# Storing the second images of the last four pairs from GpSimd's queue instead of ScalarE's

## The chip, the cores and the metric

The kernel runs on one core of a Trainium2 chip. The metric is the device time of one execution in microseconds (us); a smaller number is better. A core has five engines that work side by side: TensorE (PE, matrix products), VectorE (DVE), ScalarE (ACT), GpSimd (POOL) and SyncE (SP), and sixteen DMA engines that carry data between the device memory and the on-chip memory. SyncE, ScalarE and GpSimd can each issue DMAs, each on a queue of its own; in the profile q1 is SyncE's queue, q10 is ScalarE's, and q0, of the kind called software_dynamic, is GpSimd's.

## The reference

The kernel computes a 3x3 convolution with padding 1 on 16 images of 64 channels and 64x64 pixels, with 128 output channels, in float32:

```python
x_pad = np.pad(x, ((0, 0), (0, 0), (1, 1), (1, 1)))
for b, co, ci, kh, kw in ...:      # 16, 128, 64, 3, 3
    output[b, co] += weight[co, ci, kh, kw] * x_pad[b, ci, kh:kh+h, kw:kw+w]
```

x is 16.8 MB and the output is 33.6 MB; the weights are 0.3 MB.

## The kernel before

**Tiling.** Two images make a pair: image 0 of the pair has its 64 channels in partitions 0 to 63, image 1 in partitions 64 to 127. There are eight pairs (p = 0 to 7). A pair is worked off in four blocks (blk), each of eight row pairs, that is sixteen output rows.

**Arithmetic.** Output rows are made two at a time, j and its neighbour, with a scheme that shares one product between the two. The sums of each pair of input rows are formed beforehand (the tile ss, function sums, line 62). TensorE then computes three groups per block (function group, line 141): U, from ss with the centre weights G1; A, from single rows with G21 and G0; and Bt, from single rows with G01 and G2. ScalarE copies U out of the accumulators (the tile ut, line 182). VectorE adds A and ut into the even output rows (line 190), and Bt and ut into the odd ones (line 193). The result tile of one image of a pair is ot, 128 output channels by 64 by 64 float32, 2 MB.

**Input.** x of pairs 0 to 2 is loaded as float32 by SyncE's queue into tiles of the same pool as ot, and converted to f16 on chip by ScalarE and GpSimd. x of pairs 3 to 7 is loaded by GpSimd's queue (function load, line 56), with the conversion to f16 made by the DMA; these loads are issued early, two at about 12 us and three at about 27 us. The row sums of pairs 1 to 7 run on GpSimd (line 131), and those of pair p+1 are issued at the head of pair p's turn in the loop. The pool of ss has three buffers.

**Output.** Image 0 of a pair is stored by SyncE's queue (line 195) as soon as its last block is added. Image 1 is put on a list, held, and stored by ScalarE's queue behind ScalarE's next two copies of U (lines 184 and 185), or behind the loop (lines 198 and 199). Pairs 0 and 7 store in halves of 32 rows (pair 0 its image 0 only); all other images are stored whole. The pool of ot and of the three float32 loads has seven buffers, so a tile takes over the buffer of a tile seven earlier, after that one's store has landed.

**Order.** Instructions in keep(...) stay in the order of the program on their engine. That holds for all instructions of GpSimd and ScalarE named here. An instruction that waits, a DMA issue too, therefore holds up what stands behind it on its engine.

Of the kernel before, what the change touches and what calls it, by code (L numbers as in the profile page):

```python
# [13 lines left out]
def kernel(  # L14
# [6 lines left out]
    nc = tc.nc  # L21
# [6 lines left out]
    keep = tc.keep_in_program_order  # L28
# [27 lines left out]
    def load(p):  # L56
        xs[p] = xpool.tile([128, H, W], F16, tag="xs", name="xs")
        keep(nc.gpsimd.dma_start(xs[p], x_rows[128 * p : 128 * p + 128, :, :]))  # L58
# [3 lines left out]
    def sums(eng, p, src, lo, n):  # L62
        if p not in ss:
            ss[p] = spool.tile([128, H // 2, W], F16, tag="ss", name="ss")
        v = src.rearrange("p (j i) c -> p j i c", i=2)
        keep(
            eng.tensor_add(  # L67
                ss[p][:, lo : lo + n, :], v[:, lo : lo + n, 0, :], v[:, lo : lo + n, 1, :]
            )
        )  # L70
# [26 lines left out]
    def cast(copy, p, src, lo, hi):  # L97
        keep(copy(xs[p][:, lo:hi, :], src[:, lo:hi, :]))  # L98
# [21 lines left out]
    cuts_of = [(halves, whole)] + [(whole, whole)] * (NP - 2) + [(halves, halves)]  # L120

    def store(eng, p, b2, ot, lo, hi):
        return eng.dma_start(
            out_rows[2 * p + b2, :, lo:hi, :],
            ot.rearrange("p j i c -> p (j i) c")[:, lo:hi, :],
        )

    for p in range(NP):
        if p + 1 < NP:
            for lo in (0, 16):  # L130
                sums(nc.gpsimd, p + 1, raws.get(p + 1, xs[p + 1]), lo, 16)
                if (p, lo) == (1, 16):
                    for q in range(5, NP):
                        load(q)
        ots = [
            opool.tile([128, H // 2, 2, W], F32, tag="ot", name="ot") for _ in range(2)
        ]
        for blk in range(4):
            j0 = blk * RB

            def group(wi_rows):

                tiles = [
                    psum.tile([128, RB, W], F32, tag="acc", name="acc") for _ in range(2)
                ]
                n = 3 * len(wi_rows)
                i = 0
                for wi, off in wi_rows:
                    for kw in (1, 0, 2):
                        c_lo, c_hi = max(0, 1 - kw), min(W, W + 1 - kw)  # L150
                        for b2 in range(2):
                            p0 = 64 * b2
                            lo, hi = j0, j0 + RB
                            if off is None:
                                rhs = ss[p][p0 : p0 + 64, lo:hi, c_lo + kw - 1 : c_hi + kw - 1]
                            else:
                                while 2 * lo + off < 0:
                                    lo += 1
                                while 2 * (hi - 1) + off > H - 1:
                                    hi -= 1  # L160
                                first = 2 * lo + off
                                last = 2 * (hi - 1) + off
                                rhs = xs[p][
                                    p0 : p0 + 64,
                                    first : last + 1 : 2,
                                    c_lo + kw - 1 : c_hi + kw - 1,
                                ]
                            nc.tensor.matmul(  # L168
                                tiles[b2][:, lo - j0 : hi - j0, c_lo:c_hi],
                                Wt[p0 : p0 + 64, wi, kw, :],  # L170
                                rhs,
                                start=i == 0,
                                stop=i == n - 1,
                            )
                        i += 1
                return tiles

            U = group([(G1, None)])
            us = []
            for b2 in range(2):  # L180
                ut = upool.tile([128, RB, W], F32, tag="ut", name="ut")
                keep(nc.scalar.copy(ut, U[b2]))  # L182
                us.append(ut)
            while held and (p, blk) != (1, 0):
                keep(store(nc.scalar, *held.pop(0)))
            for piece in later.get((p, blk), ()):
                cast(nc.scalar.copy, *piece)
            A = group([(G21, 1), (G0, -1)])
            for b2 in range(2):
                nc.vector.tensor_add(ots[b2][:, j0 : j0 + RB, 0, :], A[b2], us[b2])  # L190
            Bt = group([(G01, 0), (G2, 2)])
            for b2 in range(2):
                nc.vector.tensor_add(ots[b2][:, j0 : j0 + RB, 1, :], Bt[b2], us[b2])  # L193
            if blk in cuts_of[p][0]:
                store(nc.sync, p, 0, ots[0], *cuts_of[p][0][blk])
            if blk in cuts_of[p][1]:
                held.append((p, 1, ots[1], *cuts_of[p][1][blk]))
    while held:
        keep(store(nc.scalar, *held.pop(0)))
# [30 lines left out]
```

## Time and profile before

| | us |
|---|---|
| Time of three runs: median (lowest to highest) | 126.29 (126.21 to 126.46) |
| Time of the profiled execution | 126.58 |
| Its span in the profile | 124.8 |
| First matmul on x to the last one | 9.83 to 112.6 |
| Last addition of VectorE ends | 113.98 |

DMA issues, by queue: engine, count, KB of each, and the median time from issue to landing.

```profile
out_dram<-ot ACTq DMA_DIRECT2D x7, 2048.0 KB, 19.4
out_dram<-ot SPq DMA_DIRECT2D x6, 2048.0 KB, 19.1
x<-in_x_dram SPq DMA_DIRECT2D x3, 2048.0 KB, 12.3
xs<-in_x_dram POOLq DMA_DIRECT2D x5, 1024.0 KB, 21.7
out_dram<-ot SPq DMA_DIRECT2D x4, 1024.0 KB, 11.8
out_dram<-ot ACTq DMA_DIRECT2D x2, 1024.0 KB, 10.9
```

How to read the profile: the page gives for each engine its busy time, its share of the span and the number of its instructions. The span is cut into 40 slices, and a digit is a slice's busy share in tenths, with 9 for 90% and more. A DMA queue's line gives packets, MB, and the time of its packets as a share of sixteen engines' span. The table by stretch has, for a stretch of the span, the busy time of each engine with its number of instructions in brackets, TensorE's granted clock, the DMA engines' busy share, and GB/s. In an order of time a line is start, duration, engine, line of the code, operation, output and input; in square brackets stands the idle time before it and what ended that. A name with a q (ACTq, SPq) is the engine's instruction queue, where DMA issues are recorded. The trace also has a record of each DMA packet, with its queue, start, duration and size; where the text speaks of packet records, it means these.

### The profile page before, as it was taken

How to read it: one execution, taken by the hardware profiler on the slowest of the kernel's cores; microseconds unless marked ns; L12 is line 12 of the kernel's file. 1: busy time of each engine (PE TensorE's matmuls, PEld its weight loads, DVE VectorE, ACT ScalarE, POOL GpSimd, SP SyncE). 2: the span in 40 equal slices, each digit the busy share in tenths (PEclk: the TensorE clock that was granted, in tenths of full speed). 3: DMA queues.
4: the chain of work that ended last, by engine and by line, in shares of the span. 5: the costliest groups of instructions: out<-in, count | busy, mean ns of one | idle time of the engine just before them, and what ended most of it. 6: DMA issues, size and time to landing. Idle time of an engine off the chain costs nothing.

```text
span 124.8 us, 2427 instructions
## 1 busy us (share of the span) xinstructions
PE 107.6 (86%) x984; PEld 50.2 (40%) x984; DVE 84.5 (68%) x135; ACT 46.5 (37%) x78; POOL 37.5 (30%) x28
## 2 busy tenths in 40 slices
PE   0598999999999999999999999999999999991000
PEld 0543444444444444444444444444444444440000
DVE  1009987878877887877777778777877787775000
ACT  4108649966663333333333333333333333330000
POOL 2209790899594003900066000930000000000000
PEclk9999999999999999999999999999999999999855
DMA  5999999999999999999999999999999999999991
GB/s 131 394 431 452 441 302 229 284 284 289 365 349 336 341 381 349 365 344 336 373 362 365 334 347 415 441 436 420 415 447 415 436 410 441 431 402 418 425 407 53
DMA packets 4042, 45.52 MB, mean 365 GB/s; under 512 B 448, under 2 KB 448, under 8 KB 576
## 3 DMA queue, kind: packets, MB, share of 16 engines
q1 hardware_dynamic: 2016, 23.36, 45.0%
q10 hardware_dynamic: 1296, 16.78, 31.7%
q0 software_dynamic: 720, 5.24, 20.5%
q8 instruction: 7, 0.11, 0.3%
q14 instruction: 3, 0.02, 0.0%
HBM read 17.07 MB, written 33.55 MB: 406 GB/s over the span
## 4 chain that ended last, share of the span: by engine, by line
PE 81%; DMA 6%; DVE 2%; issue 1%; DVEq 0%; SPq 0%
PE acc L168 81%; DMA x<-in_x_dram 6%; DVE ot L190 1%; DVE ss L67 1%; DVE ot L193 0%; DVEq L225 0%; SPq L41 0%; DVEq L190 0%
## 5 line engine op out<-in xcount | busy, mean ns | idle before, releaser
L168 PE MATMUL acc<-xs,Wt 64*128 64x504 f16 (+3 forms) x768 | 87.2, 373 | 0.0
L168 PEld LDWEIGHTS <-Wt 64*128 64x128 f16 x960 | 47.3, 94 | 56.2 <-issue 1.1
L182 ACT COPY ut<-acc 128x512 f32<-128x512 f32 x64 | 34.4, 589 | 56.9 <-issue 39.0
L190 DVE TENSOR_TENSOR ot<-acc,ut 128x512 f32<-128x512 f32 x64 | 41.2, 685 | 20.8 <-PE acc L168 18.4
L193 DVE TENSOR_TENSOR ot<-acc,ut 128x512 f32<-128x512 f32 x64 | 41.1, 683 | 0.0
L67 POOL TENSOR_TENSOR ss<-xs 128x1024 f16<-128x1024 f16 x10 | 21.1, 2127 | 32.6 <-DMA xs<-in_x_dram 20.5
L168 PE MATMUL acc<-ss,Wt 64*128 64x504 f16 (+1 forms) x192 | 26.1, 377 | 0.6 <-DVE ss L67 0.6
L98 ACT CAST xs<-x 128x1024 f16<-128x1024 f32 (+1 forms) x10 | 10.5, 1070 | 3.5 <-DMA x<-in_x_dram 3.5
L67 POOL TENSOR_TENSOR ss<-x 128x1024 f16<-128x1024 f32 x4 | 9.4, 2365 | 4.3 <-DMA x<-in_x_dram 4.3
L67 DVE TENSOR_TENSOR ss<-x 128x512 f16<-128x512 f32 x4 | 3.3, 867 | 7.8 <-DMA x<-in_x_dram 7.8
L85 PE MATMUL wp<-ident,w 128*64 128x128 f16 x18 | 1.3, 328 | 4.4 <-POOL w L52 4.4
L98 POOL CAST xs<-x 128x1024 f16<-128x1024 f32 (+1 forms) x2 | 3.0, 1519 | 4.7 <-DMA x<-in_x_dram 4.7
L91 PE MATMUL warm<-blank 128*128 128x400 f32 x6 | 3.6, 757 | 0.0
L85 PEld LDWEIGHTS <-w 128*64 128x64 f16 x18 | 1.1, 210 | 4.4 <-POOL w L52 4.4
L58 POOL DMA_DIRECT2D xs<-in_x_dram x5 | 2.9, 579 | 0.0
L91 PEld LDWEIGHTS warm<-blank 128*128 128x128 f32 x6 | 1.7, 304 | 1.4 <-issue 1.2
L92 ACT CAST Wt<-wp 128x384 f16<-128x384 f32 x1 | 0.5, 479 | 3.1 <-PE wp L85 3.1
L92 ACT ACT_TABLE_LOAD x1 | 1.3, 1283 | 0.7 <-PEq L214 0.7
L52 POOL CAST w<-w_raw 128x576 f16<-128x576 f32 x1 | 0.7, 662 | 2.4 <-DMA w_raw<-in_weight_dram 2.4
L88 DVE MEMSET blank<- 128x400 f32 x1 | 0.4, 392 | 0.9 <-PEq L214 0.9
L103 ACT CAST Wt<-wp 128x384 f16<-128x384 f32 x1 | 0.5, 478 | 0.5 <-DVE Wt L95 0.5
L94 DVE TENSOR_TENSOR Wt<-wp,Wt 128x384 f16<-128x384 f32 x1 | 0.6, 550 | 0.0
(8 smaller groups left out, 1.9 us busy)
## 6 DMA issues: line engine op xcount, KB each, us to landing
out_dram<-ot ACTq DMA_DIRECT2D x7, 2048.0 KB, 19.4
out_dram<-ot SPq DMA_DIRECT2D x6, 2048.0 KB, 19.1
x<-in_x_dram SPq DMA_DIRECT2D x3, 2048.0 KB, 12.3
xs<-in_x_dram POOLq DMA_DIRECT2D x5, 1024.0 KB, 21.7
out_dram<-ot SPq DMA_DIRECT2D x4, 1024.0 KB, 11.8
out_dram<-ot ACTq DMA_DIRECT2D x2, 1024.0 KB, 10.9
w_raw<-in_weight_dram SPq DMA_DIRECT2D x1, 288.0 KB, 2.9
```

Source lines behind the costliest of these rows:

```text
L52: keep(nc.gpsimd.tensor_copy(w16, w_raw))
L58: keep(nc.gpsimd.dma_start(xs[p], x_rows[128 * p : 128 * p + 128, :, :]))
L67: eng.tensor_add(ss[p][:, lo : lo + n, :], v[:, lo : lo + n, 0, :], v[:, lo : lo + n, 1, :])
L85: nc.tensor.matmul(wp[q : q + 64, k * CO : k * CO + CO], w16[:, t::9], ident)
L91: nc.tensor.matmul(warm[:, 0:400], blank[:, 0:128], blank)
L92: keep(nc.scalar.copy(wrow(G1), wps[1]))
L94: keep(nc.vector.tensor_sub(wrow(G21), wps[2], wrow(G1)))
L98: keep(copy(xs[p][:, lo:hi, :], src[:, lo:hi, :]))
L168: nc.tensor.matmul(tiles[b2][:, lo - j0 : hi - j0, c_lo:c_hi], Wt[p0 : p0 + 64, wi, kw, :], rhs, start=i == 0, stop=i == n - 1,)
L182: keep(nc.scalar.copy(ut, U[b2]))
L190: nc.vector.tensor_add(ots[b2][:, j0 : j0 + RB, 0, :], A[b2], us[b2])
L193: nc.vector.tensor_add(ots[b2][:, j0 : j0 + RB, 1, :], Bt[b2], us[b2])
```

## The change

From pair 4 on, the store of image 1 is issued by GpSimd at the place in the program where its last block is added, instead of being put on the list for ScalarE. It is kept in program order on GpSimd: the store of pair 4 stands behind the row sums of pair 5 and ahead of those of pair 6, and the store of pair 5 ahead of the row sums of pair 7. Five DMAs move: three whole images (pairs 4, 5, 6) and the two halves of pair 7. ScalarE keeps the four stores of pairs 0 to 3.

```diff
             if blk in cuts_of[p][0]:
                 store(nc.sync, p, 0, ots[0], *cuts_of[p][0][blk])
-            if blk in cuts_of[p][1]:
+            if blk in cuts_of[p][1] and p >= 4:
+                keep(store(nc.gpsimd, p, 1, ots[1], *cuts_of[p][1][blk]))
+            elif blk in cuts_of[p][1]:
                 held.append((p, 1, ots[1], *cuts_of[p][1][blk]))
     while held:
         keep(store(nc.scalar, *held.pop(0)))
```

## The prediction

> **What bounds the kernel now.** I read the head of the page first, then the DMA queues, then the busy time by stretch, and last the order of time around a pair's end and around the kernel's end.
>
> ```profile
> span 124.8 us, 2427 instructions
> PE 107.6 (86%) x984; PEld 50.2 (40%) x984; DVE 84.5 (68%) x135; ACT 46.5 (37%) x78; POOL 37.5 (30%) x28
> DMA  5999999999999999999999999999999999999991
> q1 hardware_dynamic: 2016, 23.36, 45.0%
> q10 hardware_dynamic: 1296, 16.78, 31.7%
> q0 software_dynamic: 720, 5.24, 20.5%
> ```
>
> TensorE is busy for 86% of the span, but the DMA row has a nine in every slice from the second to the last but one, and the queues' shares sum to 45.0 + 31.7 + 20.5 = 97.2% of sixteen engines' time. q1 is SyncE's queue, q10 ScalarE's, q0 GpSimd's. The table by stretch says where this decides:
>
> ```profile
> core 0: us, PE busy (x) PEld busy (x) DVE busy (x) ACT busy (x) POOL busy (x), PEclk, DMA share, GB/s
> 47.00:75.00 28.00, 28.00 (x266) 13.00 (x264) 21.96 (x36) 8.89 (x18) 8.41 (x4) 1.00 1.02 354
> 77.00:100.00 23.00, 23.00 (x218) 10.63 (x216) 18.06 (x30) 7.52 (x14) 4.21 (x2) 1.00 1.01 431
> ...
> 114.00:118.00 4.00, 0.00 (x0) 0.00 (x0) 0.00 (x0) 0.00 (x0) 0.00 (x0) 0.95 1.01 426
> 118.00:121.00 3.00, 0.00 (x0) 0.00 (x0) 0.00 (x0) 0.00 (x0) 0.00 (x0) 0.50 1.01 426
> 121.00:123.40 2.40, 0.00 (x0) 0.00 (x0) 0.00 (x0) 0.00 (x0) 0.00 (x0) 0.50 0.38 157
> ```
>
> The last two columns are the DMA engines' busy share and the GB/s that they moved. (The loads on q0 are counted at their f16 size, half of what is read, so 354 and 431 GB/s are nearly the same pace.) From 114 us no compute engine works, yet the DMA engines are full until 121. The chain of waits ends at the last addition at 113.98 us; what follows, to 124.8, is a backlog of stores. So this kernel ends when its bytes are through, about 1.4 us after its last packet: the trace's packet records put that one at 123.34 us.
>
> The order of time at a pair's end (here pair 4), and GpSimd's order around it:
>
> ```profile
> 74.28 1.28 DVE L193 TENSOR_TENSOR ot<-acc,ut 128x512 f32<-128x512 f32 x2
> ...
> 74.98 0.33 SPq L123 DMA_DIRECT2D out_dram<-ot  x1
> 75.59 0.34 ACTq L123 DMA_DIRECT2D out_dram<-ot  x1
> ```
>
> ```profile
> 26.93 1.63 POOL L58 DMA_DIRECT2D xs<-in_x_dram  x3
> ...
> 63.38 4.21 POOL L67 TENSOR_TENSOR ss<-xs 128x1024 f16<-128x1024 f16 x2 [10.37 <-PE acc L168]
> 77.98 4.21 POOL L67 TENSOR_TENSOR ss<-xs 128x1024 f16<-128x1024 f16 x2 [10.40 <-DMA xs<-in_x_dram]
> ```
>
> The first image's store leaves at 74.98, the second's at 75.59, 0.03 us after the pair's last addition. GpSimd's last two rows are the row sums of pairs 6 and 7.
>
> **The change part by part.** The sum is made against the profiled execution: 126.58 us, of which 124.8 are span and 1.8 lie around it. The median of the runs shown is 126.29, which is 0.29 less; I carry differences over to it.
>
> *Five store issues leave ScalarE*, 0.34 us each. After each of them ScalarE sat idle for 2.1 us before its next copy (78.08 after 75.59, 90.89 after 88.39, 103.70 after 101.20). Worth: 0. That cover is the wait for TensorE's next block, and nothing in the change touches it.
>
> *Five store issues come to GpSimd.* The five loads that it issues took 0.579 us on average (535 to 704 ns), so 2.9 us in all, on an engine busy for 30%. What matters is what stands behind them. The store of pair 4 waits for 75.56 and stands ahead of pair 6's sums, which ran at 63.38: they move to 75.56 + 0.6 = 76.2 and end at 80.4. Pair 5's store waits for 88.37 and stands ahead of pair 7's sums: 89.0 to 93.2 instead of 77.98 to 82.2. TensorE reads them first at 86.83 and 99.64 (the first matmuls on ss of those pairs). Both have 6.4 us to spare, so 0; with that cover gone, each us would hold up TensorE by one. Pairs 6 and 7's stores have no sums behind them.
>
> *Output buffers.* The transfers issued by 75.6 us all land by 94.51 now. With the same bytes on the same engines, another order between queues can't finish the whole later, and the last two tiles that need a freed buffer are first written at 101.75. Worth 0, with 7 us to spare.
>
> *Issue to first packet.* With the engines full, a queue that was empty starts late whoever owns it. From the packet records: ScalarE's queue 26.96 to 30.62 (3.66 us) and 101.20 to 105.17 (3.97), SyncE's 106.96 to 111.28 (4.32), GpSimd's 12.05 to 15.91 (3.86, descriptor writing included). So a moved store starts between 0.5 us earlier and 0.2 us later than on ScalarE's queue. It costs only where an engine runs dry. In the records the number of packets in flight never falls under 16 between 3 and 121 us. The tightest spot is the end: the last half image needs 8 packets of 0.309 us per engine, 2.47 us, and the engines finish between 121.28 and 123.34, so they are out of other work between 118.8 and 120.9. Its first packet can come at 113.98 + 4.32 = 118.3. Covered on every engine, by 2.6 us on the one that sets the end: 0.
>
> *The packets themselves.* 512 packets of 16 KB (or their worth) change queue, 32 per engine. Upper bound: by the queues' shares, q0's packets took 0.205 x 16 x 124.8 / 640 = 640 ns each and q10's 0.317 x 1996.8 / 1024 = 618 ns per 16 KB, 22 ns more, which gives 32 x 22 ns = 0.70 us. But q0's loads also convert to f16, and packets overlap. The pace tells more: with three queues sharing, ScalarE's stores land 14.67 us apart (56.93, 71.60), that is 24 packets per engine at 611 ns; with two queues, 9.71 us (91.69, 101.40) for 16, at 607. If q0 alone is charged with the 4 ns, 8 of its packets cost 0.10 us and 32 cost 0.40. Lower bound: nothing, if the conversion explains it; the bytes are the same, so below nothing is excluded for this term. By rate of bytes read, in the packet records, 47 to 75 us ran at 427.0 GB/s and 77 to 100 us at 429.1, 0.5% apart; over the 44 us in which stores would be on q0 that is 0.2 us. I take half of it, 0.1, as the rate is nearer to "no difference" than to 0.70.
>
> *The end.* SyncE waits for all landings; after the last one 1.4 us pass. Unchanged.
>
> Sum: 0 + 0 + 0 + 0 + 0.1 = +0.1, so 126.68 against the profiled 126.58, and **126.4 us** against the median of 126.29: the same, if no change is taken as within 0.2% (0.25 us), about what a measurement of this kernel can resolve.
>
> **The rivals.** *A queue that is slow when it is alone* (slower). Load 3 is the only transfer that ever had engines to itself on q0. While it shared with SyncE's load its packets took 625 ns; from 19.2 to 22.7 us, when that load had ended, 60 of them took 758 ns on average, up to 1132. ScalarE's queue, nearly alone from 108 to 111 us, kept a median of 611. If the cause is the software queue, it returns where q0 will be alone: now q10 is alone for about 28 engine-us at 108 to 111 (38.1 busy less 9.9 of q1 beside it) and 15 at 118 to 123.4, 2.7 us per engine. At 758/611, 24% more: +0.65 us, **127.0**. If it is the conversion, or reading x, nothing. It decides from about 0.9 us per engine with q0 alone. One stretch is thin evidence, and q0's later packets at 28 to 30 us, when they held 12 of 16 engines between 8 KB stores, took 624.
>
> The Trainium skill ("DMA: Bandwidth & Descriptors", section Bandwidth) gives 425 GB/s for a 16 MB load issued from GpSimd; by that a software queue alone would not be slow, and no run here shows an unconverted GpSimd transfer.
>
> *Two slow engines set the end* (slower). If two of the sixteen engines lag whenever q0 runs, the last store's slowest share ends later. The spread between the first and the last engine's completion was 0.78 us for the load that ended before q0 started and 2.37 for the next, +1.6, which would give 126.3 + 1.6 = **127.9**. Against it: through loads 5 to 7 it stayed at 2.77, 2.77 and 2.59, and ScalarE's stores, with q0 gone, show 2.20, 2.82, 2.04; it doesn't grow with q0's packets.
>
> The Trainium skill ("DMA: Bandwidth & Descriptors", section Latency and other measured facts) has a rule of this kind: engines 7 and 15 are usually slower, by its best guess because of the software descriptor rings; by the rows above this trace agrees with it at most once.
>
> *The last store comes too late* (slower). If an issue on GpSimd took over 6.8 us from the last addition to its first packet, the engine that sets the end would run dry at 120.9; each us beyond adds one, so at 8 us **127.5**. The row for GpSimd says 3.9.
>
> *A more even finish* (faster). The engines end between 121.28 and 123.34, on average at 122.06. If the software queue dealt rows out so that the slowest engine had less, up to 1.28 us could go; half of it gives **125.7**. Against it: both kinds of queue show 144 packets per transfer (720/5, 1296/9), 128 rows and 16 completions, so equal shares per engine.
>
> **How the numbers follow.** Forecast (no change; its own range 126.05 to 126.54): 0.45. Slow when alone: 0.25. Two slow engines: 0.06. Late last store: 0.08. More even finish: 0.14. An unnamed small loss: 0.02. So faster 0.14, same 0.45, slower 0.41. The range, 126.0 to 127.2, takes in the forecast, the 0.70 bound and the slow queue; it leaves out about 0.1 below (most of the even finish) and 0.1 above (the slow engines, most of the late store, the far end of the slow queue).
>
> **What would show it.** Right: five store issues on GpSimd of about 0.6 us, at 75.6, 88.4, 101.2, 107.6 and 114.0; sums of pairs 6 and 7 at about 76 and 89; matmuls unbroken to 112.6; DMA share at 1.0 until 121; q0 at 10 transfers, 13.6 MB; last packet at about 123.4. Wrong: idle time of TensorE before its matmuls on ss at 86.8 or 99.6; GB/s under 420 in 80 to 121 us; a DMA share under 0.95 at 104 to 111 or 114 to 121; a spread of the last completions well over 2.1 us.

## The result, and the profile after

Over 14 runs of each kernel the median went from 126.33 us (126.17 to 126.66) to 126.65 us (126.50 to 127.24). The ratio is 1.0028 with a 95% interval of 1.0020 to 1.0037: slower by about 0.35 us, a little more than the 0.2% under which the prediction spoke of no change. The time lies inside the predicted range of 126.0 to 127.2; the likeliest single case, no change, just missed.

The two profiled executions can't show this by their times: 126.55 us after, 126.58 before. They show it by their parts. The head of the page and the DMA queues of the changed kernel:

```profile
span 124.7 us, 2423 instructions
PE 107.7 (86%) x984; PEld 50.2 (40%) x984; DVE 84.5 (68%) x135; ACT 46.5 (37%) x78; POOL 40.3 (32%) x33
DMA  5999999999999999999999999999999999999991
q1 hardware_dynamic: 2016, 23.36, 45.0%
q0 software_dynamic: 1440, 13.63, 36.4%
q10 hardware_dynamic: 576, 8.39, 15.8%
```

Five transfers have gone from q10 to q0, nothing else has moved, and the DMA row is as full as it was. By stretch (engines' busy times, granted clock, DMA share, GB/s):

```profile
47.00:75.00 28.00, 28.00 (x266) 12.94 (x262) 22.07 (x36) 8.89 (x18) 4.20 (x2) 1.00 1.02 355
77.00:100.00 23.00, 23.00 (x220) 10.61 (x216) 18.06 (x30) 7.52 (x14) 8.34 (x5) 1.00 1.01 431
...
118.00:121.00 3.00, 0.00 (x0) 0.00 (x0) 0.00 (x0) 0.00 (x0) 0.00 (x0) 0.50 1.01 426
121.00:123.40 2.40, 0.00 (x0) 0.00 (x0) 0.00 (x0) 0.00 (x0) 0.00 (x0) 0.50 0.42 174
```

In the first three rows 355, 431 and 426 GB/s stand where there were 354, 431 and 426: the bytes move at the old pace. GpSimd's order of time shows the moved work where it was expected:

```profile
75.75 0.58 POOL L123 DMA_DIRECT2D out_dram<-ot  x1 [22.69 <-DVE ot L193]
76.35 4.20 POOL L67 TENSOR_TENSOR ss<-xs 128x1024 f16<-128x1024 f16 x2
88.56 0.58 POOL L123 DMA_DIRECT2D out_dram<-ot  x1 [8.01 <-DVE ot L193]
89.16 4.21 POOL L67 TENSOR_TENSOR ss<-xs 128x1024 f16<-128x1024 f16 x2
...
114.17 0.53 POOL L123 DMA_DIRECT2D out_dram<-ot  x1 [5.91 <-DVE ot L193]
```

What differs lies behind the last byte. By the packet records the last packet ends at 123.06 us (123.35 before), but the span goes on to 124.74 (124.77). From the last packet to the end of the span, which I call the tail, it took 1.42 us before and takes 1.69 now, **0.27 us more**. The instructions of the program's end are listed under its last line (L225 before, L227 after): count, shortest, median and longest in ns, first and last start in us.

```profile
L225 SPq EVENT_SEMAPHORE  x10: 17/28/28, 113.8 to 124.7; - x10
L225 POOLq DRAIN  x3: 39/93/4692, 78.0 to 124.5; - x3
L225 SPq DRAIN  x3: 7/7/7, 124.0 to 124.3; - x3
```

```profile
L227 SPq EVENT_SEMAPHORE  x11: 17/28/1349, 115.3 to 124.7; - x11
L227 POOLq DRAIN  x3: 45/93/9830, 114.1 to 124.5; - x3
L227 SPq DRAIN  x3: 7/7/7, 123.8 to 124.2; - x3
```

GpSimd closes with a drain. Before, it began at 78.0, when its last sums were under way, and was long over at the end. Now it begins at 114.1 and lasts 9.83 us, to 123.98, which is 0.92 us behind the last packet; SyncE's own closing waits were over at 123.83, and the closing barrier, at 124.02, waits for both. That gave the first theory.

### The profile page after: what moved, and what is told of

Same layout as the page of the kernel before. It is cut to its first block, busy times and chain, and to the rows that moved or that the text cites. A ratio compares the mean times of both kernels' runs of the same rounds, so it can differ in the third digit from the quotient of the medians.

```text
span 124.7 us, 2423 instructions
## 1 busy us (share of the span) xinstructions
PE 107.7 (86%) x984; PEld 50.2 (40%) x984; DVE 84.5 (68%) x135; ACT 46.5 (37%) x78; POOL 40.3 (32%) x33
## 4 chain that ended last, share of the span: by engine, by line
PE 76%; DMA 6%; issue 6%; DVE 2%; POOLq 0%; POOL 0%; SPq 0%; DVEq 0%
PE acc L168 76%; DMA x<-in_x_dram 6%; DVE ot L193 1%; DVE ot L190 1%; DVE ss L67 1%; POOLq L227 0%; POOL out_dram L123 0%; SPq L41 0%; DVEq L190 0%
## 5 line engine op out<-in xcount | busy, mean ns | idle before, releaser
L123 POOL DMA_DIRECT2D out_dram<-ot x5 | 2.8, 558 | 50.4 <-DVE ot L193 50.4
```

The source lines that it names most:

```text
L123: return eng.dma_start(out_rows[2 * p + b2, :, lo:hi, :], ot.rearrange("p j i c -> p (j i) c")[:, lo:hi, :],)
```

## The experiments

All runs below stand beside runs of the kernel before on the same chip; a run's ratio is its time over theirs, with the 95% interval in brackets. In theory A GpSimd's drain is the cost; in theory B the software queue moves bytes more slowly; theory C is mere scatter in where the sixteen engines finish.

**The changed kernel again (e1).**

> The changed kernel once more, beside the kernel before, to have its loss against the same runs as the others. All theories: 0.2 to 0.45 us slower than before. Theory A (the end of the program costs it: GpSimd's closing drain lasts until its own last store has landed and is over after SyncE's): from the last DMA packet to the end of the span 1.65 to 1.75 us, against 1.43 before. Theory B (the software queue moves its bytes more slowly): the tail is 1.43 and the last packet comes 0.3 us later than before. Theory C (noise between executions of where the DMA engines finish): the last packet varies by some tenths of a us in both directions.

Measured: 1.0017 (0.9999 to 1.0035), tail 1.69 us, last packet at 123.28. The tail is that of the first profile to 0.01 us. The times go from 126.38 to 127.13, but for one of 128.44; without that one their median is 126.67, 0.35 above before. The interval just holds no change.

**All but the last moved store on GpSimd (e2).**

```diff
-            if blk in cuts_of[p][1] and p >= 4:
+            if blk in cuts_of[p][1] and p >= 4 and (p, blk) != (NP - 1, 3):
```

> As the changed kernel, but the very last store (image 1 of pair 7, second half) is ScalarE's again, so four of the five moved transfers, 7.3 of 8.4 MB, stay on GpSimd. Theory A: the loss is gone, within 0.12 us of before; GpSimd's closing drain ends by 120.5 us, ahead of the last landing, and the tail is 1.40 to 1.50 us. Theory B: seven eighths of the loss stay, 0.2 to 0.35 us slower than before.

Measured: 1.0034 (1.0016 to 1.0053). The loss stayed, against theory A. But theory B gets no support either, since the tail did not go back: 1.72 us, although the drain was over early.

```profile
L227 SPq EVENT_SEMAPHORE  x11: 17/28/28, 115.4 to 125.7; - x11
L227 POOLq DRAIN  x3: 45/93/14240, 108.0 to 125.5; - x3
L227 SPq DRAIN  x3: 7/7/7, 125.0 to 125.3; - x3
```

GpSimd's long drain ran from 107.96 to 122.20. SyncE was now the late one: its closing waits were over at 125.03, 2.8 us later and 0.97 us behind the last packet, which in this execution of 127.56 us ended at 124.06. So something besides the drain makes the tail.

**Only the last store on GpSimd (e3).**

```diff
-            if blk in cuts_of[p][1]:
+            if blk in cuts_of[p][1] and (p, blk) == (NP - 1, 3):
+                keep(store(nc.gpsimd, p, 1, ots[1], *cuts_of[p][1][blk]))
+            elif blk in cuts_of[p][1]:
```

> As the kernel before, but only the very last store (image 1 of pair 7, second half, 1 MB) is GpSimd's. Theory A: nearly the whole loss, 0.2 to 0.35 us slower than before, with a tail of 1.65 to 1.75 us and a drain on GpSimd that ends 0.9 us after the last packet. Theory B: one eighth of the loss, at most 0.05 us slower.

Measured: 1.0024 (1.0011 to 1.0038), tail 1.66 us, last packet 123.30. One eighth of the bytes brings about as large a loss as all of them; one per byte would have been 0.05 us, and the interval begins at 0.14. So the cost isn't one per byte. But the drain ended 0.63 us behind the last packet, earlier than SyncE's closing waits at 0.89, so here too it wasn't the drain that ended last.

**The last two stores change queues (e4).**

```diff
+            if (p, blk) == (NP - 1, 3):
+                keep(store(nc.gpsimd, p, 0, ots[0], *cuts_of[p][0][blk]))
+                store(nc.sync, p, 1, ots[1], *cuts_of[p][1][blk])
+                continue
             if blk in cuts_of[p][0]:
```

> As the changed kernel, but in the last block of pair 7 the two images change queues: GpSimd stores the second half of image 0, SyncE that of image 1. GpSimd has as many bytes as in the changed kernel, but its last store is issued 0.6 us earlier and need not be the last to land. Theory A: if SyncE's store lands last, by 0.5 us or more, the loss is gone or falls to 0.1 us; if GpSimd's still lands last, the loss stays 0.25. Theory B: 0.2 to 0.45 us slower, as the changed kernel.

Measured: 1.0044 (1.0022 to 1.0065), tail 1.68. GpSimd's store, though issued first, still landed last (123.18 against 122.88), so this run tells little.

**A new theory, from SyncE's closing list.** A semaphore is a counter; the trace shows each DMA raise one by 16 as it lands. The trace's instruction records show what SyncE does at the end: it waits for the semaphores of all DMAs, and of some engines, in a fixed order, mostly two in one instruction, 0.06 us apart when nothing has to be waited for. The order, with the semaphores' numbers: 101; 102 and 110; 103 and 109; 114 and 108; 115 and 107; 116 and 106; 117 and 100; 118 and 105; in kernels with three or more stores on GpSimd, 113 and 112 come first and 111 goes with 101; in e3, with one, only 111 joins. DMAs of the two hardware queues take the eight semaphores 101 to 103 and 114 to 118 by turns in the order of issue; GpSimd's use 106 to 113. Before, the kernel's 23 hardware DMAs ended with the last store on 117, with one wait behind it. Moving five of them shifts every later one: in e2 the last two stores use 102 and 103, with up to six waits behind, and in the changed kernel GpSimd's last store uses 107, with three behind. There the wait for 107 ended at 123.55, the three others began at 123.58, 123.64 and 123.71, and SyncE's first two closing drains at 123.77 and 123.83. Theory D: the tail is 1.35 us and 0.06 more for each wait that stands behind the last landing, or the drain, if that ends later.

**Split stores, to shift the turns (e5 to e7).** These were to set the turn of the last stores by splitting early ones into 112 and 16 output channels, two DMAs for one. The diff is e7's, which splits pair 1; e6 splits pairs 1 and 2, and e5, on top of e2, pairs 1 to 4.

```diff
             if blk in cuts_of[p][0]:
-                store(nc.sync, p, 0, ots[0], *cuts_of[p][0][blk])
+                if p == 1:
+                    flat = ots[0].rearrange("p j i c -> p (j i) c")
+                    for c0, c1 in ((0, 112), (112, 128)):
+                        nc.sync.dma_start(out_rows[2 * p, c0:c1], flat[c0:c1])
+                else:
+                    store(nc.sync, p, 0, ots[0], *cuts_of[p][0][blk])
```

> As e2 (four of the moved stores on GpSimd, the last one on ScalarE), but the stores of image 0 of pairs 1 to 4 are issued as two DMAs each, 112 and 16 output channels, so that the last two stores are again the 22nd and 23rd of the hardware queues' DMAs and use the semaphores that SyncE's closing list waits for near its end, as in the kernel before. Theory D (what costs is the end: after the last landing SyncE still goes through the waits that stand later in its list, 0.06 us each, seven of them in e2 against one before, and where GpSimd issued the last store its drain): tail 1.40 to 1.50 us, time within 0.12 us of before. Theory B (stores on the software queue are dearer): the tail is 1.42 and the time still 0.25 to 0.4 us longer, with the last packet later by as much.

> As the kernel before, nothing on GpSimd's queue but its loads; the stores of image 0 of pairs 1 and 2 are issued as two DMAs each, 112 and 16 output channels. That makes 25 DMAs on the hardware queues in place of 23, and the last store then uses the semaphore that stands first in SyncE's closing list. Theory D: the tail grows from 1.42 to 1.75 to 1.9 us and the time by 0.3 to 0.45, without any store on GpSimd. Theories A and B: the tail stays 1.42 and the time within 0.1 us of before.

> As e6, but pair 1 alone is split: 24 DMAs, the last store on the semaphore that stands last in SyncE's list. Theory D: the tail is 1.33 to 1.42 us and the time within 0.1 us of before, so that e6's loss is not that of splitting a store. If splitting itself costs, half of e6's loss is here.

Measured: e5 1.1367 (1.1330 to 1.1403), e6 1.0753 (1.0703 to 1.0803), e7 1.0382 (1.0336 to 1.0429). The splits themselves cost 4 to 5 us each, so the times say nothing on theory D. The tails do, since they begin behind the last packet: 1.47 us in e5 (last landing on 116), 1.81 in e6 (101), 1.39 in e7 (118). Theory D had 1.40 to 1.50, 1.75 to 1.9 and 1.33 to 1.42. What the split did is told in the last section.

**Both images of the last four pairs on GpSimd (e8).**

```diff
             if blk in cuts_of[p][0]:
-                store(nc.sync, p, 0, ots[0], *cuts_of[p][0][blk])
+                if p >= 4:
+                    keep(store(nc.gpsimd, p, 0, ots[0], *cuts_of[p][0][blk]))
+                else:
+                    store(nc.sync, p, 0, ots[0], *cuts_of[p][0][blk])
```

> As the changed kernel, but image 0 of the last four pairs is stored by GpSimd too, so 16.8 MB in place of 8.4 go through the software queue, and from about 85 us on it is the only one in use. Theory B: the last packet comes 0.4 us or more later than before and the loss doubles, to 0.5 us or more. A queue that is slow when alone: as worked out in the prediction, a quarter more per packet over the last 35 us, up to 8 us. Theory D: last packet as before, tail 1.6 to 1.9 us, loss 0.2 to 0.45 us.

Measured: 1.0077 (1.0055 to 1.0099), tail 1.77 us, last packet 123.92. The loss is more than double, which is theory B's number; what the run shows is something else. By stretch:

```profile
77.00:85.00 8.00, 8.00 (x78) 3.62 (x75) 6.55 (x12) 2.15 (x4) 4.09 (x2) 1.00 1.01 430
85.00:100.00 15.00, 15.00 (x144) 6.92 (x142) 11.52 (x20) 5.37 (x10) 5.32 (x4) 1.00 1.01 428
100.00:104.00 4.00, 4.00 (x42) 1.86 (x40) 3.42 (x6) 1.07 (x2) 1.10 (x2) 1.00 0.91 377
```

With q0 the only queue in use from 87 us on (the others' last stores end at 84.2 and 86.6), the engines moved 428 GB/s, and the median packet took 611 ns. So the software queue alone was not slow here. The Trainium skill ("DMA: Bandwidth & Descriptors", section Bandwidth) has 425 GB/s for a 16 MB load issued from GpSimd; this run agrees, for stores, with 428. What e8 loses in the bytes, it loses at 101 to 103 us, where the engines had worked off pair 5 and pair 6's stores were not yet there: counted in the packet records, 6.2 engine-us idle, 0.4 us per engine, against 0.04 engine-us before and none in the changed kernel. The tail is 0.36 us longer. Another 0.4 us lies outside the profiled span, ahead of the first instruction or behind the last: time less span is 2.16 to 2.23 us in all six executions of e8, and 1.75 to 1.84 in the eleven of before beside it. The three make up the 1.08 us by which the median is longer, to within 0.1. Why the time outside the span grew, no trace shows; in the other runs it did not.

**The turns shifted without splits (e9, e10).** A DMA of 64 bytes into a tile that nothing reads takes a turn too. The diff is e9's; e10 has one in place of two.

```diff
+    for k in range(2):
+        crumb = const.tile([1, 16], F32, name=f"crumb{k}")
+        nc.sync.dma_start(crumb, w_flat[k : k + 1, 0:16])
     raws = {1: x1, 2: x2}
```

> As the kernel before, with two more DMAs on SyncE's queue behind the loads of x, each of 64 bytes into a tile that nothing reads. They move no work worth naming, but make 25 DMAs on the hardware queues, so that the last store uses the semaphore that stands first in SyncE's closing list, as in e6, without split stores. Theory D: last packet as before, tail 1.75 to 1.85 us, time 0.3 to 0.5 us longer than before, with nothing of the change in it. Otherwise: tail 1.42, no change within 0.1 us.

> The same with one such DMA: 24 on the hardware queues, the last store on the last semaphore of the list. Theory D: tail 1.33 to 1.42 us, time within 0.1 us of before, perhaps 0.05 shorter. If the small DMA itself costs, half of e9's loss is here.

Measured: e9 1.0036 (1.0018 to 1.0053), tail 1.77; e10 1.0022 (0.9998 to 1.0045), tail 1.35. e9 has no store on GpSimd and loses about as much as the changed kernel. SyncE's waits for DMAs at the end (total us, number, longest), first e9, then e10:

```profile
SPq L228 <- DMA out_dram<-ot: 9.9, 1, 9.9
```

```profile
SPq L228 <- DMA out_dram<-ot: 9.1, 5, 3.5
```

In e9 SyncE sits in one wait until the last store has landed, and goes through all the others after that; in e10 it takes them one by one as they land, and the last landing is the last item. The first of its closing drains (the first start in each line) came 0.97 us behind the last packet in e9, which ended at 123.31, and 0.55 in e10, at 123.06:

```profile
L228 SPq DRAIN  x3: 7/7/7, 124.3 to 124.6; - x3
```

```profile
L228 SPq DRAIN  x3: 7/7/7, 123.6 to 123.9; - x3
```

e10's time is inconclusive: its median is 126.43 against 126.27, and its interval holds both nothing and 0.4%. Half of e9's 0.31 us is here too, which is what was expected if a small DMA itself costs something. So the tails of the two are theory D's; the times don't separate it from that rival.

**Stores on GpSimd with the old turns (e11, e12).** e11 is e2 with four such DMAs; e12 moves only the whole images of pairs 4 to 6, with three.

> As e2 (four of the five moved stores on GpSimd, the last one on ScalarE) with four such DMAs, so that the last stores are the 22nd and 23rd of the hardware queues as in the kernel before. Theory D alone: tail 1.40 to 1.50, time within 0.1 us of before. If the stores on the software queue cost something besides: the tail is the same and the time stays 0.1 to 0.3 us longer.

> Only the whole second images of pairs 4, 5 and 6 on GpSimd, both halves of pair 7 on ScalarE, with three such DMAs, so that the last store is again the 23rd of the hardware queues. Theory D alone: tail 1.40 to 1.50, time within 0.1 us of before. If the software queue's stores cost besides, three quarters of what e11 shows stays.

Measured: e11 1.0024 (1.0011 to 1.0037), tail 1.43; e12 1.0017 (1.0004 to 1.0030), tail 1.61. e11's tail is that of the kernel before to 0.01 us, with 7.3 MB of stores still on GpSimd. e12's expected 1.40 to 1.50 was missed: both hardware queues ended at 123.07, and the last landing was not on its semaphore until 0.65 us behind the packet, where it took 0.47 before. The medians did not follow the tails all the way: they stay 0.27 and 0.20 us above before, and both intervals lie above no change.

The tails together: the number of waits that stand in SyncE's list behind the last landing, how long behind the last packet that landing was on its semaphore, the tail, the median's distance from that of before, and the quickest execution.

| kernel | waits behind | landing us | tail us | median above before, us | quickest us |
|---|---|---|---|---|---|
| e10 | 0 | 0.46 | 1.35 | 0.16 | 126.14 |
| before | 1 | 0.47 | 1.42 | 0 | 126.08 |
| e11 | 1 | 0.46 | 1.43 | 0.27 | 126.21 |
| e12 | 1 | 0.65 | 1.61 | 0.20 | 126.29 |
| after; e1 | 3, and the drain | 0.47 | 1.69; 1.69 | 0.32; 0.35 | 126.50; 126.38 |
| e4 | 3, and the drain | 0.46 | 1.68 | 0.53 | 126.57 |
| e2 | 6 | 0.46 | 1.72 | 0.44 | 126.50 |
| e3 | 7 | 0.34 | 1.66 | 0.36 | 126.54 |
| e9 | 7 | 0.46 | 1.77 | 0.31 | 126.50 |

From e10 to e9, (1.77 - 1.35) / 7 = 0.06 us per wait. Take the landing and 0.06 us for each wait from the tail, and 0.89 to 0.90 us are left in each of the ten profiles in which SyncE ended last (e5, e6 and e7 among them). In after, e1 and e4, in which GpSimd's drain ended last, 1.04 us are left, and 0.95 in e8, with eight waits behind, where the drain was the last by less. That also accounts for the two tails that miss theory D's numbers, e3's and e12's: they differ in the landing. What sets a landing's delay stays open.

The times follow less closely. The quickest executions fall into two groups: up to 126.29 with tails to 1.61, from 126.38 with tails from 1.66; but 126.08 is the lowest of more than thirty, the others of 11 to 14. From e2 to e11 the tail falls by 0.30 us and the median's distance by 0.17; from e9 to e10 by 0.42 and 0.15. The ratios' intervals overlap in both pairs.

## Why the prediction was right or wrong

*ScalarE's five issues, worth 0:* right; its busy time is 46.5 us in both.

*GpSimd's five issues and the sums behind them, worth 0:* right. The issues took 0.558 us each (0.579 had been taken), the sums of pairs 6 and 7 started at 76.35 and 89.16 (76.2 and 89.0), and TensorE ran on without a gap.

*Output buffers, worth 0:* right; nothing waited for one.

*Issue to first packet:* the size was off, the verdict held. Pair 4's store took from 75.75 to 80.07, 4.3 us, and pair 6's from 101.37 to 106.38, 5.0, where 3.9 to 4.3 had been taken. The last half image's first packet came at 119.04, where 118.3 had been taken. No engine ran dry there: the DMA share is 1.01 until 121. But the tightest spot is not the end, as I had it: it is 101 to 103 us, as e8 shows. Even before, 16 packets were not always in flight there, as I had read; the number fell to 14, with 0.04 engine-us lost.

*The packets themselves, +0.1:* not shown. q0's stores took 617 ns per 16 KB on average; q10's before, from 75.6 us on, took 617 too, so the 22 ns that the queues' shares gave did not return with the stores. The time of all packets, per engine, sums to 121.51 us before, 121.61 after and 121.59 in e1; but it is 121.74 in e9, which has no store on q0, and 121.51 in e12, which has 6.3 MB there. A tenth of a us can't be told from scatter by these.

*The end, "unchanged":* this is the step that failed. I read "SyncE waits for all landings" as one wait whose length depends on the last landing alone. It is a list. The change moved the last landing from a place with one wait behind it to a place with three behind it, and put a drain of GpSimd beside it. In the changed kernel the list took SyncE 0.10 us longer behind the last packet (0.77 against 0.67), and the drain ended another 0.15 later: with rounding, 0.27 us in the tail of the profile. The loss by the ratio is about 0.35.

*The rivals.* The queue that is slow when alone is refuted by e8's 428 GB/s; whether load 3's slow packets came of its conversion or of that moment stays open. The two slow engines are refuted by the finish: on average over the engines, counted from the idle time behind 118 us, 122.17 us against 122.09 before, and a spread of 1.56 us for the last store against 2.07. A late last store, with engines dry at the end, did not happen. The more even finish is half there in this profile (last packet 0.30 us earlier), but not as a rule: over the profiles of before, after, e1, e3 and e4 the last packet lies between 123.06 and 123.35 with no order in it.

What is shown: the tail grew by 0.27 us in both profiles of the changed kernel, and waits and drain account for it; e9 makes as large a tail, and about as large a loss, without the change; e3 makes them with one store. That the tail is most of the lost time is argued from the profiles, not shown by the times. In the two profiled executions the longer tail is balanced by a last packet 0.30 us earlier. And e11 keeps 0.27 us of the median with the tail of before. The small DMAs may cost that much (e10, with one and no store on GpSimd, has 0.16 too many), or it may be the scatter of the sixteen engines' finish (one engine of e2 finished 1.8 us behind the average), or a small cost of the software queue; these runs don't tell them apart. That the predicted range held is in part luck: +0.1 stood in the sum for the packets, and what came was in the end, which had been put at nothing. No kernel tried beat the kernel before.

## What to carry to other kernels

When a kernel ends in a backlog of transfers, as this one does, ask first whether another queue moves the bytes faster or slower; here it did neither. Then look at what comes behind the last byte: which engine's closing instructions end last, and how many waits stand behind the last landing in the list. In these kernels adding or moving a DMA shifted the tail by up to 0.4 us, so a difference of 0.3% between two of them needs the tail measured before the edit is blamed or praised. And a store from GpSimd that lands last can bring GpSimd's closing drain onto the path, as in the changed kernel; in e3 it did not, since more waits of SyncE stood behind.

## What the hardware showed unexpectedly

A store split by partitions, 112 and 16 channels in place of 128, hardly changed the number of packets and none of the bytes. By the ratios it cost 4.8 us (e7), 9.5 (e6, two splits) and, with e2's change, 17.3 (e5, four). The same stretch before and in e7:

```profile
40.00:64.00 24.00, 24.00 (x230) 11.10 (x226) 18.36 (x30) 8.26 (x16) 4.83 (x3) 1.00 1.02 357
```

```profile
40.00:64.00 24.00, 24.00 (x230) 10.77 (x226) 18.36 (x30) 8.50 (x16) 4.21 (x2) 1.00 1.01 305
```

The DMA engines are as busy as before and move 305 GB/s in place of 357. In the packet records, 47 of the 350 packets of 16 KB that the two hardware queues began in this stretch took over 1 us, up to 3.3; before it was one of 418, with 1.02; the loads on q0 kept their 0.62 at the median. Why the packets slow one another when a store is split so, these runs don't show.
